# A hybrid attention layer on one core: TensorE's order pinned to the program through the attention stages

## The chip, the cores and the metric

The kernel runs on one core of a Trainium2 chip. The metric is the time of one execution on the device in microseconds (us), lower is better; the times shown are the median of several executions. Five engines work side by side, each in the order of its own queue: PE (TensorE: matmuls and transposes), DVE (VectorE), ACT (ScalarE), POOL (GpSimd) and SP (SyncE, which issues most DMAs). Where one needs another's result it waits on a semaphore.

## The reference

One decoder layer on x of 512 tokens by 2048, in float32. Each of the 8 FoX heads does softmax attention with a forgetting bias; the 8 NSA heads (two groups that share keys) mix three branches by sigmoid gates: attention over 31 compressed blocks, over selected blocks (all of them here, since 512 tokens have 8 blocks and 16 are taken) and over a window.

```python
def reference(x, ...):
    h = _rms_norm(x, attn_norm)
    x = x + _hybrid_mixer(h, ...)      # proj = h @ w_in, cut into qf, kf, vf, ff, qn, kc, vc, ks, vs, kw, vw, gt
    h = _rms_norm(x, ffn_norm)         # heads are RMS-normed, attended, concatenated, multiplied by w_out
    return x + (silu(h @ w_gate) * (h @ w_up)) @ w_down
```

## The kernel before, in words

Tokens lie along the free axis (512), features on the 128 partitions. Every float32 operand is split into a high and a low half, and every product is three matmuls: high by high, high by low and low by high (`mm3`, or the three calls in `unit`). ACT writes the high half (a copy that rounds), DVE the low one (`split`, `load_w`): so each weight part costs a load, an ACT pass and a DVE pass before PE can use all of it.

The work comes in four stages.

- *First projection* (5 to 50 us): x and the weights of kc and vc arrive in 16 steps `k`; each step makes `bigm` (x, split), `w0p` (the weight, split) and 12 matmuls of 512 columns into four banks `ps_first`. Squares of x are summed in `acc` for the norm; `ps_r` sums them over partitions, `rstd` is worked out by ACT and DVE, and `ps_rT` transposes it (`token_rstd`, called by `unload`).
- *Woven stage* (50 to 640 us): 20 units of the input projection (`ps_ks`, `ps_fg`, `ps_qn`, `ps_vs`, `ps_qf`, ...). `stream(units)` yields after every 6 matmuls of 256 columns, and `weave` steps side work in between at places that the list `plan` writes down: (first step, last step, how many, generator). Side work is the unloading of the first banks, the compressed keys and values (`z_kc`, `zkT`, `z_vc`), the gates with the cumulated forgetting (`ps_cum`), the normed and transposed heads (`nT_...`), and the attention branches: scores (`s_...`, `m_s`), transposed probabilities (`pT_...`, split into `pt_...`) and products with the values (`o_...`). Letters: f is FoX, s selected, w window; `s_f73` is head 7, query block 3.
- *Output projection* (640 to 664 us): `first_outs` fills `po0` and `po8`, with the last two heads woven in by a second `plan`.
- *The rest of the output projection, norm and feed-forward* (664 us to the end): here PE's order, ACT's and DVE's are already those of the program. The last pass ends in `finish(q, b)`, four times: DVE scales two banks by rstd (`t4_q`, `t62_q`; the profile drops the digits and calls them t) and adds them to the kept sums (`ca` is `y[1]`, `cb` is `y[0]`), whose halves are then stored.

A tile scheduler sets the order in each engine's queue. An instruction that went through `keep_in_program_order` (also as `pin`, while `pinned[0]` is set, and as `inorder` and `order0`) keeps its place among the other such instructions of its engine; one that did not is placed where the scheduler takes it to be ready. Before, PE's instructions of the first three stages are left to the scheduler, but for the warm-up and step k = 0; so are most of ACT's and DVE's, but for the weight halves and the first readers of projection banks. A psum bank of tag "g" or "t" has two buffers, so a matmul that starts a bank waits until the one two before has been read.

The code that the change touches:

## Time and profile before

| | |
|---|---|
| median of 3 runs | 2094.19 us (2093.47 to 2094.68) |
| profiled execution | 2093.31 us, of which the span of the trace is 2091.6 |
| PE busy | 99% of the span, 16935 matmuls and transposes |
| DVE busy | 79% |
| ACT busy | 46% |
| POOL busy | 9% |

Rows of the timeline read: start and duration in us, engine, line, operation, output<-input by the program's names without their numbers, shapes, xcount (several in one row), and in brackets the idle time ahead with the instruction that ended it. Rows of the list of waits read: engine, what waited, what it waited for, total us, times, longest. Matmuls overlap: their cost is the distance of their starts, not their duration.

### The profile page before, as it was taken

The page shows a single profiled execution, that of the slowest core. Times are in us where ns is not written, and L with a number is a line of the kernel's source. Part 1 is how long each engine was busy: PE and PEld are TensorE (multiplying, and loading weights), DVE is VectorE, ACT ScalarE, POOL GpSimd, SP SyncE. Part 2 cuts the span into 40 slices and gives each one's busy share as a digit, 9 for nine tenths or more (in the row PEclk, how much of TensorE's full clock was granted, in tenths as well). Part 3 has the DMA queues.
Part 4 walks back from the last instruction along what each step waited for, and adds up shares of the span by engine and source line. Part 5 has one row for each costly group of instructions (what it writes and reads, how often), then busy time and mean ns, then how long its engine had stood idle before and what let it go on. Part 6 is the DMA issues. An engine that isn't in the chain of part 4 may idle for free.

```text
span 2091.6 us, 40521 instructions
## 1 busy us (share of the span) xinstructions
PE 2079.4 (99%) x16935; PEld 2025.5 (97%) x16935; DVE 1648.8 (79%) x2437; ACT 966.6 (46%) x1226; POOL 181.8 (9%) x297
## 2 busy tenths in 40 slices
PE   9999999999999999999999999999999999999998
PEld 7999999999998888999999999999999999999998
DVE  6757667554456455999999999999999987889898
ACT  6445555444345334443344344433433455565553
POOL 1000000010010000111111111111111000000000
PEclk9999999999999999999999999999999999999999
DMA  5521211222223444667767767777777797579864
GB/s 202 172 87 51 71 52 61 81 95 81 94 82 106 151 143 141 174 198 193 198 190 187 194 189 196 197 180 204 189 185 200 243 337 248 153 240 331 290 179 139
DMA packets 113496, 350.58 MB, mean 168 GB/s; under 512 B 13592, under 2 KB 13848, under 8 KB 113312
## 3 DMA queue, kind: packets, MB, share of 16 engines
q1 hardware_dynamic: 85408, 270.98, 38.7%
q0 software_dynamic: 22144, 52.44, 14.2%
q10 hardware_dynamic: 5760, 24.57, 3.0%
q8 instruction: 132, 2.16, 0.4%
q14 instruction: 52, 0.43, 0.1%
HBM read 319.35 MB, written 74.73 MB: 188 GB/s over the span
## 4 chain that ended last, share of the span: by engine, by line
PE 93%; DVE 3%; ACT 2%; issue 1%; DMA 0%; SPq 0%; DVEq 0%; ACTq 0%
PE q L1182 39%; PE pd L1324 13%; PE pd L1329 6%; PE ps_qf L280 3%; PE ps_qf L283 3%; PE ps_qf L282 3%; PE po L166 3%; PE po L168 3%; PE po L167 3%; PE ps_vf L280 1%; PE ps_vf L283 1%; PE ps_vf L282 1%; PE ps_qn L280 1%; PE ps_qn L282 1%; PE ps_qn L283 1%
## 5 line engine op out<-in xcount | busy, mean ns | idle before, releaser
L83 ACT ACTIVATE bigm<-r 128x1792 fp32r<-128x1792 f32 x174 | 298.2, 1714 | 466.5 <-PE q L1182 296.9
L80 DVE TENSOR_TENSOR bigm<-r,bigm 128x1792 fp32r<-128x1792 f32 x174 | 351.4, 2020 | 11.6 <-ACT bigm L83 11.0
L80 DVE TENSOR_TENSOR r<-r 128x512 f32<-128x512 f32 x522 | 267.2, 512 | 29.2 <-DMA r<-wgu 16.8
L1182 PE MATMUL q<-bigm 128*128 128x256 f32 x1848 | 218.0, 277 | 0.1
L1182 PE MATMUL q<-forma,bigm 128*128 128x256 f32 x1848 | 216.9, 276 | 0.0
L1182 PE MATMUL q<-formy,bigm 128*128 128x256 f32 x1848 | 216.8, 276 | 0.0
L1182 PE MATMUL q<-formx,bigm 128*128 128x256 f32 x1848 | 216.8, 276 | 0.0
L1182 PEld LDWEIGHTS q<-bigm 128*128 128x128 f32 x1848 | 213.8, 188 | 0.3 <-DVE bigm L80 0.3
L1182 PEld LDWEIGHTS q<-forma,bigm 128*128 128x128 f32 x1848 | 213.1, 188 | 0.1
L1182 PEld LDWEIGHTS q<-formy,bigm 128*128 128x128 f32 x1848 | 212.9, 188 | 0.1
L1182 PEld LDWEIGHTS q<-formx,bigm 128*128 128x128 f32 x1848 | 212.9, 188 | 0.0
L125 POOL DMA_DIRECT2D wsum<-wdn x176 | 119.8, 687 | 863.9 <-ACT bigm L83 760.2
L280 PE MATMUL ps_qf<-wp_qf,bigm 128*128 128x256 f32 x512 | 145.1, 283 | 0.0
L283 PE MATMUL ps_qf<-wp_qf,bigm 128*128 128x256 f32 x512 | 142.3, 278 | 0.0
L282 PE MATMUL ps_qf<-wp_qf,bigm 128*128 128x256 f32 x512 | 142.3, 278 | 0.0
L1324 PE MATMUL pd<-bigm 128*128 128x256 f32 x1176 | 141.8, 276 | 0.0
L1324 PEld LDWEIGHTS pd<-bigm 128*128 128x128 f32 x1176 | 137.3, 188 | 0.0
L80 DVE TENSOR_TENSOR bigm<-wd,bigm 128x2048 fp32r<-128x2048 f32 (+1 forms) x64 | 110.2, 1723 | 12.2 <-ACT bigm L83 11.9
L83 ACT ACTIVATE bigm<-rawm 128x768 fp32r<-128x768 f32 (+2 forms) x72 | 65.9, 925 | 108.2 <-PE pd L1329 59.6
L166 PE MATMUL po<-bigm,wp_o 128*128 128x512 f32 x256 | 100.0, 390 | 0.0
L167 PE MATMUL po<-bigm,wp_o 128*128 128x512 f32 x256 | 99.8, 390 | 0.0
L168 PE MATMUL po<-bigm,wp_o 128*128 128x512 f32 x256 | 99.7, 390 | 0.0
(450 smaller groups left out, 4427.0 us busy)
## 6 DMA issues: line engine op xcount, KB each, us to landing
r<-wgu SPq DMA_DIRECT2D x174, 512.0 KB, 4.5
wsum<-wdn POOLq DMA_DIRECT2D x176, 256.0 KB, 4.9
rawm<-ad SPq DMA_DIRECT2D x44, 512.0 KB, 7.1
wd<-wdn SPq DMA_DIRECT2D x40, 512.0 KB, 6.0
wd<-wsum SPq DMA_DIRECT2D x40, 512.0 KB, 6.9
ad<-cb ACTq DMA_DIRECT2D x22, 896.0 KB, 5.7
rawm<-ad SPq DMA_DIRECT2D x44, 384.0 KB, 3.4
ws_qf<-win SPq DMA_DIRECT2D x32, 512.0 KB, 3.3
```

The costliest lines, as they stand in the source:

```text
L80: return pin(nc.vector.tensor_tensor(*args, op=op))
L83: return pin(nc.scalar.activation(*args, **kw))
L125: d = nc.gpsimd.dma_start(step[0], step[1], **step[2])
L166: nc.tensor.matmul(o, lh, rh, start=start, stop=False)
L167: nc.tensor.matmul(o, lh, rl, start=False, stop=False)
L168: nc.tensor.matmul(o, ll, rh, start=False, stop=stop)
L280: nc.tensor.matmul(o, xg[k][:, 0, c], wp[:, 0, w], start=(k == 0 and b == 0), stop=False, skip_group_check=True)
L282: nc.tensor.matmul(o, xg[k][:, 0, c], wp[:, 1, w], start=False, stop=False, skip_group_check=True)
L283: nc.tensor.matmul(o, xg[k][:, 1, c], wp[:, 0, w], start=False, stop=(k == NK - 1), skip_group_check=True)
L1182: nc.tensor.matmul(o, w[wp][:, fb, cs], a[:, xp, fa], start=(k == 0 and h == 0 and wp == 0 and xp == 0), stop=(g == NG - 1 and kk == 1 and ...
L1324: nc.tensor.matmul(b[q][k][:, h * 256:(h + 1) * 256], w[0][:, fb, q * P:(q + 1) * P], a[xp][:, fa], start=(j == 0 and h == 0 and xp == 0), ...
L1329: nc.tensor.matmul(b[q][k][:, h * 256:(h + 1) * 256], w[1][:, fb, q * P:(q + 1) * P], a[0][:, fa], start=False, stop=(j == NJ - 1), skip_g ...
```

## The change

It pins PE's order from the start of the woven stage to the end of the last attention branch: `mm3` and all matmuls and transposes of these stages now go through wrappers that keep the order of the program while `pe_pinned[0]` is set. Beside that ("all of the former"): x_0 and the first weights are loaded ahead of everything but the vector of gains; in steps k > 0 of the first projection, the split of x and w and the squares are pinned on ACT and DVE; `gneg` is worked out in step 1 instead of before the first step; the zeroing of a strip of `xb` is pinned; the first entry of `plan` starts one step later; and in `finish` the subtraction on `ca` goes to GpSimd for the first two passes, with the first addition on `cb` ahead of the store of `ca`.

```diff
+    pe_pinned = [False]
+
+    def pe_matmul(*args, **kw):
+        m = nc.tensor.matmul(*args, **kw)
+        return tc.keep_in_program_order(m) if pe_pinned[0] else m
+
+    def pe_transpose(*args, **kw):
+        m = nc.tensor.transpose(*args, **kw)
+        return tc.keep_in_program_order(m) if pe_pinned[0] else m
+
     def mm3(o, lh, ll, rh, rl, start, stop):
-        nc.tensor.matmul(o, lh, rh, start=start, stop=False)
+        pe_matmul(o, lh, rh, start=start, stop=False)
...
+    x0 = oxp.tile([P, T], F32, tag="ox", name="x_0", bufs=NOX)
     nc.scalar.dma_start(vt, vec)
+    nc.sync.dma_start(x0, xT[0])
+    early = oxp.tile([P, 5 * T], F32, tag="x5", name="early")
+    nc.sync.dma_start(early[:, :T], wfirst[0])
...
     gneg = ap_.tile([P, 2], F32, name="gneg")
-    nc.vector.tensor_scalar_mul(gneg[:, 0:1], v1(V_FQ), -SCALE)
-    nc.vector.tensor_scalar_mul(gneg[:, 1:2], v1(V_NQ), -SCALE)
...
-                nc.vector.tensor_scalar_mul(xb[:, 4 * T:4 * T + 16], ident[:, :16], 0.0)
+                inorder(nc.vector.tensor_scalar_mul(xb[:, 4 * T:4 * T + 16], ident[:, :16], 0.0))
...
-            nc.scalar.activation(sq, xs, AF.Square)
-            nc.vector.tensor_tensor(acc, acc, sq, op=OP.add)
+            pin(nc.scalar.activation(sq, xs, AF.Square))
+            pin(nc.vector.tensor_tensor(acc, acc, sq, op=OP.add))
...
-            split(t, xs, v1(V_AN + k))
+            pinned[0] = True
+            g = v1(V_AN + k)
+            pin(nc.scalar.activation(t[:, 0], xs, AF.Copy, scale=g))
+            pin(nc.vector.scalar_tensor_tensor(t[:, 1], xs, g, t[:, 0].bitcast(F32), op0=OP.mult, op1=OP.subtract))
             split(wp[:, :, :T], ws)
...
             square(k, xs)
+            if k == 1:
+                pin(nc.vector.tensor_scalar_mul(gneg[:, 0:1], v1(V_FQ), -SCALE))
+                pin(nc.vector.tensor_scalar_mul(gneg[:, 1:2], v1(V_NQ), -SCALE))
+            pinned[0] = False
...
-    plan = [(2, 30, 9, chain(unload(), windows("kc", V_PK))), (26, 42, 4, windows("vc", V_PV)),
+    plan = [(3, 30, 9, chain(unload(), windows("kc", V_PK))), (26, 42, 4, windows("vc", V_PV)),
...
+    pe_pinned[0] = True
     weave(stream(units), plan)
...
     weave(first_outs(), plan)
     run(rest)
+    pe_pinned[0] = False
...
-        tt(y[1], y[1], t4, op=OP.subtract)
-        fetch2(out[n + 1], y[1])
-        tt(y[0][:, :256], y[0][:, :256], t4[:, :256], op=OP.add)
+        pin((nc.gpsimd if q < 2 else nc.vector).tensor_tensor(y[1], y[1], t4, op=OP.subtract))
+        tt(y[0][:, :256], y[0][:, :256], t4[:, :256], op=OP.add)
+        fetch2(out[n + 1], y[1])
```

The number of instructions does not change on PE. Its order changes at some fifteen places; three of all the places, as the queues of the two kernels have them (line, operation, output<-input, shape, count):

PE, in the unit fg (the gate weights `wp_fg`, second part), before: seven matmuls of the compressed keys, then the first matmuls of four banks, which need the high half of the part alone, then the transposes of the normed ks0 and kw0, and only then a matmul with the low half (line 282).

```order
L528 MATMUL z_kc_860<-wp_kc0_863,xb_kc_701 128x256 x3
L528 MATMUL z_kc_860<-wp_kc1_905,xb_kc_701 128x256 x4
L280 MATMUL ps_fg0_827<-wp_fg_1_833,bigm_76 128x288
L280 MATMUL ps_fg1_828<-wp_fg_1_833,bigm_76 128x288
L280 MATMUL ps_fg2_829<-wp_fg_1_833,bigm_76 128x288
L280 MATMUL ps_fg3_830<-wp_fg_1_833,bigm_76 128x288
L340 MATMUL nT_ks0_986<-ident_124,t_ks0_533 128x128 x4
L340 MATMUL nT_kw0_1012<-ident_124,t_ks0_533 128x128 x4
L282 MATMUL ps_fg0_827<-wp_fg_1_833,bigm_76 128x288
```

The same place now; all wrapped matmuls have the line of the wrapper:

```order
L168 MATMUL ps_fg3_830<-wp_fg_0_742,bigm_76 128x288 x6
L168 MATMUL z_kc_860<-wp_kc0_863,xb_kc_701 128x256
L168 MATMUL ps_fg0_827<-wp_fg_1_833,bigm_76 128x288 x6
L168 MATMUL z_kc_860<-wp_kc0_863,xb_kc_701 128x256
L168 MATMUL ps_fg1_828<-wp_fg_1_833,bigm_76 128x288 x6
L168 MATMUL z_kc_860<-wp_kc0_863,xb_kc_701 128x256
L168 MATMUL ps_fg2_829<-wp_fg_1_833,bigm_76 128x288 x6
L168 MATMUL z_kc_860<-wp_kc1_905,xb_kc_701 128x256
```

One z_kc matmul stands ahead of the second part, and the second matmul of that part comes right behind its first; the other z_kc matmuls follow one by one, and nT_ks0 and nT_kw0 come two parts later.

PE, in the output projection, before: the transposes `nT_kf7` of the last key head, and the scores of its query block 3 (`s_f73`, three matmuls: high, and with the low halves), the two behind each other only in part.

```order
L340 MATMUL nT_kf7_7586<-ident_124,t_qf7_7248 128x128 x4
L166 MATMUL po8_7540<-bigm_76,wp_o8_0_7580 128x512
L465 MATMUL pT_f60_7607<-ident_124,p_f6_7127 128x128 x4
L167 MATMUL po8_7540<-bigm_76,wp_o8_0_7580 128x512
L166 MATMUL s_f73_7600<-qf7_7567 128x512
L168 MATMUL po8_7540<-bigm_76,wp_o8_0_7580 128x512
L166 MATMUL po8_7540<-bigm_76,wp_o8_0_7580 128x512
L167 MATMUL po8_7540<-bigm_76,wp_o8_0_7580 128x512
L168 MATMUL po8_7540<-bigm_76,wp_o8_0_7580 128x512
L166 MATMUL s_f72_7625<-qf7_7567 128x384
L166 MATMUL po8_7540<-bigm_76,wp_o8_0_7580 128x512
L167 MATMUL s_f73_7600<-qf7_7567 128x512
```

The same place now:

```order
L168 MATMUL po8_7540<-bigm_76,wp_o8_0_7580 128x512 x3
L172 MATMUL nT_kf7_7586<-ident_128,t_qf7_7248 128x128 x4
L168 MATMUL s_f73_7600<-qf7_7567 128x512 x3
L172 MATMUL pT_f60_7607<-ident_128,p_f6_7127 128x128 x4
L168 MATMUL po8_7540<-bigm_76,wp_o8_0_7580 128x512 x6
L168 MATMUL s_f72_7625<-qf7_7567 128x384 x3
L172 MATMUL pT_f61_7631<-ident_128,p_f6_7127 128x128 x4
```

The scores follow their transposes at once; pT_f60 and the matmuls of po8 stand behind them.

DVE, in the tail, before, in the first pass of `finish` and the start of the second:

```order
L80 TENSOR_TENSOR t4_0_22905<-pd30_1_21981,rstd_134 128x512
L80 TENSOR_TENSOR ca_8848<-ca_8848,t4_0_22905 128x512
L80 TENSOR_TENSOR cb_8846<-cb_8846,t4_0_22905 128x256
L80 TENSOR_TENSOR t62_0_22906<-pd30_0_21980,rstd_134 128x512
L80 TENSOR_TENSOR cb_8846<-cb_8846,t62_0_22906 128x512
L80 TENSOR_TENSOR t4_1_22941<-pd31_1_21983,rstd_134 128x512
```

And the end of POOL's queue now, behind the loads of x1:

```order
L1251 DMA ca_8848<-x1d13_7827 128x512
L1251 DMA cb_8846<-x1d14_7828 128x512
L1251 DMA ca_8848<-x1d15_7829 128x512
L1291 TENSOR_TENSOR ca_8848<-ca_8848,t4_0_22905 128x512
L1291 TENSOR_TENSOR ca_8848<-ca_8848,t4_1_22941 128x512
```

The subtractions on ca of the first two passes have left DVE's queue and are the last two instructions of POOL's.

## The prediction

> **What bounds the kernel now.** I read the head of the page first (span, busy time, granted clock, the chain that ended last), then the list of waits on PE, then a table of busy time by stretches, and last the timeline at every place where the change gives PE another order.

> ```profile
> span 2091.6 us, 40521 instructions
> PE 2079.4 (99%) x16935; PEld 2025.5 (97%) x16935; DVE 1648.8 (79%) x2437; ACT 966.6 (46%) x1226; POOL 181.8 (9%) x297
> PEclk9999999999999999999999999999999999999999
> PE 93%; DVE 3%; ACT 2%; issue 1%; DMA 0%; SPq 0%; DVEq 0%; ACTq 0%
> ...
> PE warm L753 <- DVE ones L210: 1.4, 1, 1.4
> PE ps_qn L282 <- DVE wp_qn L149: 1.0, 1, 1.0
> PE ps_first L168 <- DVE w0p L80: 0.7, 1, 0.7
> ...
> PE ps_rT L257 <- DVE rstd L218: 0.4, 1, 0.4
> PE pT_s L465 <- DVE pt_s L80: 0.3, 1, 0.3
> PE ps_qn L280 <- DVE vs L364: 0.2, 1, 0.2
> ...
> 50.00:120.00 70.00, 68.58 (x552) 66.50 (x551) 49.98 (x87) 34.22 (x61) 1.15 (x1) 1.00 0.50 163
> 664.00:2050.00 1386.00, 1385.88 (x11496) 1358.10 (x11496) 1208.41 (x1494) 626.76 (x537) 134.54 (x199) 1.00 0.70 204
> ```

> PE is busy 99% of the span at full granted clock and carries 93% of the chain. Its waits are few, and none before the tail is longer than 1.4 us. So the instruction count of PE (unchanged) sets the time, and all that the change can do up to the tail is to take away some of these few waits or to make new ones. In the table (length; busy time of PE, weight loads, DVE, ACT, POOL; clock; DMA) the feed-forward stretch from 664 to 2050 us has PE idle 0.1 us in 1386: it will only be shifted. DVE is busy 50.0 of 70 us in the stretch from 50 to 120: it is no bound, but its results often come just in time.

> **The change part by part.** The two orders of PE agree nearly everywhere. They differ at about fifteen places, and these have one form: before, PE had other ready work in front of an instruction whose input was late; in the order of the program that work stands behind it. What it costs is the moved work, as long as the late input comes at the same time as before. A projection matmul of 256 columns costs the distance of two starts, 0.113 us:

> ```profile
> 54.55 0.28 PE L280 MATMUL ps_ks<-wp_ks,bigm 128*128 128x256 f32 x1
> 54.66 0.28 PE L282 MATMUL ps_ks<-wp_ks,bigm 128*128 128x256 f32 x1
> 55.32 0.63 PE L257 MATMUL ps_rT<-ident,rstd 128*128 128x128 f32 x4 [0.38 <-DVE rstd L218]
> ...
> 54.48 0.69 DVE L218 TENSOR_TENSOR rstd<-rstd,tmp_r 128x512 f32<-128x512 f32 x1
> ```

> *rT.* The transposes of rstd come when DVE's row at 54.48 ends (55.17). Before, 32 matmuls lie between the sums of squares and them, now 18. The 14 that covered the wait are done afterwards: 14 x 0.113 = **+1.6**.

> *Gates and first compressed keys.* DVE makes the low half of the second part of the gate weights late, because a scaling of t_ks (1.22 us) stands ahead of it:

> ```profile
> 76.82 0.99 PE L528 MATMUL z_kc<-wp_kc,xb_kc 128*128 128x256 f32 x7
> 78.14 1.22 DVE L327 TENSOR_TENSOR t_ks<-t_ks,sn_ks 128x1024 f32<-128x1024 f32 x1
> 79.28 1.82 DVE L149 TENSOR_TENSOR wp_fg<-ws_fg,wp_fg 128x768 fp32r<-128x768 f32 x2
> 79.42 0.33 PE L340 MATMUL nT_ks<-ident,t_ks 128*128 128x128 f32 x1 [0.60 <-DVE t_ks L327]
> ```

> Until about 80.2 (79.28 and half of 1.82) PE had seven z_kc matmuls, four high-half gate matmuls and eight transposes to do. In the new order it can do one z_kc and one gate matmul. Six z_kc at 0.118 ((0.99 - 0.28)/6), three gate matmuls at 0.13 (0.113 x 288/256) and eight transposes at 0.10 (four took 0.63 in the rT row and one 0.33 here) move behind: 0.71 + 0.39 + 0.80 = **+1.9**. PE then stands still for some 3 us, in two pieces.

> *zkT, then the cumulated gates.* zkT waited 0.18 us for DVE; now 12 fewer matmuls lie ahead of it (1.36). ps_cum needs the triangle that DVE casts until 111.71; 5 of the 11 matmuls that covered this go (0.57). Together **+1.9**.

> ```profile
> 110.11 0.27 PE L544 MATMUL zkT<-ident,zks 64*128 64x64 f32 x1 [0.18 <-DVE zks L541]
> 111.28 0.43 DVE L620 CAST tri<-trif 128x512 fp32r<-128x512 f32 x1
> 154.47 1.26 DVE L452 TENSOR_SCALAR p_s<-p_s,st_s 128x512 f32<-128x512 f32 x4
> 209.17 0.30 PE L565 MATMUL m_s<-Kc,qn 128*128 128x64 f32 x1 [0.22 <-DVE st_s L442]
> 275.74 0.88 DVE L364 SCALAR_TENSOR_TENSOR vs<-ps_vs,rT,vs 128x256 fp32r<-128x256 f32 x2
> 276.28 0.39 PE L280 MATMUL ps_qn<-wp_qn,bigm 128*128 128x256 f32 x1 [0.25 <-DVE vs L364]
> ```

> *Third compressed score (row at 209.17).* It already waited; it now follows 12 instead of 24 matmuls: 12 x 0.113 = **+1.4**.

> *First part of qn6 (276.28).* Its bank is free when DVE has read vs. Before, three score matmuls of 512 columns, three of 384, three products of 256 and seven transposes ran ahead of it, now behind: 0.69 + 0.52 + 0.34 + 0.70 = 2.25, by the distances given here and below. In the new DVE order the reads of that bank stand together, without the masking of another score (some 0.7) between them: **+1.5**.

> *Small ones.* pT_s0 loses five covering matmuls (DVE's four scalings end at 155.73): 0.55. m_s1 loses three: 0.35. z_vc and m_s0: 0.3. **+1.2**.

> *Output projection with the last heads.*

> ```profile
> 644.17 1.22 DVE L327 TENSOR_TENSOR t_qf<-t_qf,sn_qf 128x1024 f32<-128x1024 f32 x1
> 648.96 0.74 DVE L138 SCALAR_TENSOR_TENSOR qf<-nT_kf,vt,qf 128x512 fp32r<-128x512 f32 x1
> 650.09 0.39 PE L167 MATMUL s_f<-qf 128*128 128x512 f32 x1
> 659.08 0.39 PE L167 MATMUL po<-bigm,wp_o 128*128 128x512 f32 x1
> 659.31 0.40 PE L168 MATMUL po<-bigm,wp_o 128*128 128x512 f32 x1
> 660.19 1.28 DVE L80 TENSOR_TENSOR pt_f<-pT_f,pt_f 128x512 fp32r<-128x512 f32 x2
> 660.93 0.44 PE L465 MATMUL pT_f<-ident,p_f 128*128 128x128 f32 x2
> ```

> Wide matmuls start 0.23 apart (659.08, 659.31). nT_qf stands two of them earlier: 0.45. s_f73 needs both halves of qf, the low one at 649.70 by DVE's row at 648.96; before, seven wide matmuls, a transpose group and single score matmuls ran there, now the three score matmuls come right behind nT_kf: I take 1.6, of 0.4 to 2.2. pT_f72 waits for a bank that DVE frees in the row at 660.19, behind three instead of nine wide matmuls: 6 x 0.23 = 1.4. Together **+3.45**.

> *First projection.* PE lost 0.7 us where DVE was late with w0p:

> ```profile
> 10.10 2.04 POOL L641 TENSOR_SCALAR nb<-nb 128x512 f32<-128x512 f32 x2
> 13.62 1.09 DVE L80 TENSOR_TENSOR w0p<-early,w0p 128x512 fp32r<-128x512 f32 x1
> 14.63 0.68 DVE L761 TENSOR_TENSOR acc<-acc,sq 128x512 f32<-128x512 f32 x1
> ```

> DVE's 128x512 takes 1.09 us while POOL works and 0.68 after it. The pinned order puts the weight split ahead of the sum of squares, and POOL's masks can start earlier, when DVE has little to do. I take **-0.9** (the wait and its restart); ends 0 and -1.1. The first loads go out in the same order as before; the squares that ACT now does in order have cover, since an x tile has 8 buffers.

> *Tail.* After the last matmul (about 2085.5) DVE works alone:

> ```profile
> 2077.16 0.69 DVE L80 TENSOR_TENSOR ca<-ca,t 128x512 f32<-128x512 f32 x1
> 2077.76 0.42 DVE L80 TENSOR_TENSOR cb<-cb,t 128x256 f32<-128x256 f32 x1
> 2085.30 0.28 PE L1347 MATMUL pd<-formx,bigm 128*128 128x256 f32 x1
> 2087.07 0.69 DVE L80 TENSOR_TENSOR t<-pd,rstd 128x512 f32<-128x512 f32 x1
> ```

> Two subtractions on ca go to POOL. DVE's rows follow each other without a gap there, so its chain gives up 2 x 0.60 (2077.16 to 2077.76) = 1.2; PE's end caps it at 2087.07 - 2085.58 = 1.5. POOL's price for this is not in the trace; its 128x512 tensor-scalar took 1.02 beside DVE (half of 2.04). While it works, DVE pays up to 0.41 an instruction (1.09 - 0.68), for three or four: the gain lies between 1.2 and -0.4. I take the middle, **-0.6**. DVE's t of the third pass also waits until POOL has read the first t; that is 4 us later. The store of ca now waits for POOL, long before the end. If DVE stood still through both POOL rows, 2 x 1.02 would be lost against 1.2, and the tail would be 0.8 longer. [...]

> *Sum.* 1.6 + 1.9 + 1.9 + 1.4 + 1.5 + 1.2 + 3.45 - 0.9 - 0.6 = +11.4. PE's later waits on DVE in the list (1.0, 0.3, 0.2 and a few like them, some 1.9 us) shrink if PE comes later and DVE doesn't; I take 1.9 off: **+9.5**. The profiled execution lasted 2093.31, 1.7 more than its span and 0.9 less than the median of the three runs, so 2094.2 + 9.5 = **2103.7**. Loads of weights are cast three buffers ahead and a later PE only gives them time.

> **The rivals.**
> *DVE runs ahead, and half of it vanishes.* While PE stands, ACT and DVE go on with weight splits that don't need PE. Each stall then makes the next input relatively early. The terms whose late input sits in DVE's queue behind such work (gates 1.9, third score 1.4, qn6 1.5, pT_f72 1.4, pT_s0 0.55) are 6.75; without them +2.75, or 2096.9, no change to be measured. For it: DVE has 20 us of slack in the 70 to 120. Against: in rT, zkT and s_f73 the late input is a chain from PE's own result, and it starts no earlier.
> *Faster.* If all inputs were there by the time the program calls for them, no new wait comes, and the old ones (0.7, 0.6, 0.4, 0.3, 0.2 and the 1.0) go, with 1.2 in the tail: -4.4, 2089.8. This decides only if DVE is earlier by 2 us at the gates and at 648.96, and nothing in the change takes work from its queue there.
> *The throttle.* The clock was granted in full in all 40 slices, with no wait above 1.4 us; the stands would now reach 3 us at the gates in two pieces, 1.5 to 2 at qn6 and s_f73. If the clock falls to half after such a stand, for as long again as PE stood there, these three lose half of 6.5 us more: 3.2, or 2106.9. Against it: behind each stand PE is at once busy again, and no row shows the clock react. [...]

> **How the numbers follow.** A measurement of this kernel can't tell less than 0.2%, 4.2 us: 2090.0 to 2098.4 is no change. The forecast (most of the sum stays, 2098.4 to 2106.5) 0.70; the sum in full or a little more, to 2108, 0.06; the throttle (some of it in the range) 0.04; half or less 0.14; faster 0.06. So slower 0.80, same 0.14, faster 0.06. The range 2096.5 to 2107.5 leaves out the faster case, the lower half of the "same" case and the throttle: some 0.17. Its lower end is the first rival; its upper end the sum without the 1.9 taken off, and with the tail and the first projection at nothing (2094.2 + 12.9 = 2107.1).

> **What would show it.** The list of waits on PE should now name rT with some 2 us (from 0.4), fg with 2 to 3 in two pieces, zkT, m_s and qn (on vs) with 1.3 to 2 each, s_f with 1.5 to 2, pT_f with 1.4, and ps_first should be gone from it. PE's busy time should stay at 2079, and the stretch from 664 to 2050 should keep its length. In the last stretch two POOL rows on ca should appear, with DVE rows near 1.1 beside them if they contend. I am wrong if DVE's rows at these places come earlier by as much as PE is, or if waits elsewhere shrink by more than 1.9.

## The result, and the profile after

The changed kernel takes 2109.22 us (median of 6 runs, 2108.55 to 2111.88) against 2094.19 before: ratio 1.0072, 95% interval 1.0062 to 1.0082. That is 15.0 us slower; 9.5 were forecast, and the range ended at 2107.5. The direction was right and the size was not. The profiled execution took 2109.01 with a span of 2107.3. In two of the experiments below, three executions (2140.45, 2126.98 and 2126.96 us) lay 1.7% above the fastest of their kernel at the same mean clock; the medians leave them out.

The head of the page of the changed kernel:

```profile
span 2107.3 us, 40543 instructions
PE 2082.9 (99%) x16935; PEld 2029.2 (96%) x16935; DVE 1649.4 (78%) x2435; ACT 968.0 (46%) x1226; POOL 182.9 (9%) x299
```

Its list of waits on PE (what waited, for what; total us, times, longest):

```profile
PE ps_qn L168 <- DVE vs L376: 2.6, 1, 2.6
PE ps_rT L269 <- DVE rstd L232: 2.0, 1, 2.0
PE ps_fg L168 <- DVE wp_fg L149: 1.9, 1, 1.9
PE m_s L168 <- DVE st_s L454: 1.9, 2, 1.6
PE zkT L172 <- DVE zks L553: 1.5, 1, 1.5
...
PE pT_f L172 <- DVE pt_f L80: 1.2, 1, 1.2
PE ps_qn L168 <- DVE wp_qn L149: 1.0, 1, 1.0
PE s_f L168 <- ACT qf L137: 0.8, 1, 0.8
PE s_f L168 <- DVE qf L138: 0.7, 1, 0.7
```

The new waits are those that were foretold, place by place, and ps_first is gone. But PE's busy time rose by 3.5 us with the same 16935 instructions, and the prediction had it staying at 2079. The table by stretches (length; busy time of PE, weight loads, DVE, ACT, POOL; granted clock; DMA) says where:

```profile
50.00:120.00 70.00, 63.15 (x493) 61.12 (x492) 47.99 (x86) 32.47 (x59) 1.15 (x1) 0.98 0.46 151
120.00:300.00 180.00, 173.56 (x1382) 168.43 (x1381) 115.05 (x299) 91.15 (x218) 8.96 (x15) 0.99 0.19 63
664.00:2050.00 1386.00, 1384.77 (x11437) 1354.99 (x11436) 1201.27 (x1498) 624.97 (x542) 134.25 (x201) 1.00 0.69 203
```

The clock fell to 0.98 and 0.99 on the mean. The forty slices of the page hid it: a slice is 53 us. The same table, cut where the clock rows of the trace change, in pairs (a stretch of 3.41 us, the first one cut short by 0.05, and the next one), and two more stretches of that grid:

```profile
78.00:81.36 3.36, 0.97 (x5) 0.55 (x5) 3.26 (x8) 1.58 (x3) 0.00 (x0) 1.00 0.22 78
81.36:84.77 3.41, 3.41 (x16) 3.41 (x16) 0.70 (x1) 0.27 (x1) 0.00 (x0) 0.50 0.71 216
282.75:286.16 3.41, 0.97 (x8) 0.97 (x9) 1.45 (x4) 2.28 (x6) 0.00 (x0) 1.00 0.00 0
286.16:289.57 3.41, 3.41 (x19) 3.41 (x18) 1.62 (x2) 1.31 (x2) 0.00 (x0) 0.50 0.13 19
112.08:115.49 3.41, 1.87 (x15) 1.58 (x13) 3.35 (x14) 1.43 (x8) 1.00 (x1) 1.00 0.43 153
214.48:217.89 3.41, 1.83 (x16) 1.63 (x15) 2.85 (x13) 1.19 (x5) 0.00 (x0) 1.00 0.36 125
```

Behind the stands at the gates (81 us) and at the first part of qn6 (286 us) the clock was halved for 3.41 us each. By the granted 0.50, as an estimate, PE did in them what takes 1.7 us: twice 1.7 us lost. (From 286.52 us one projection matmul took 0.42 us and four 1.06, so they start 0.213 apart, against 0.113 at full clock; by these it is 1.6.) Behind the stands at zkT (112) and the third compressed score (214), where PE was busy 1.83 us or more of the 3.41, it was not.

For the terms I took the distance in time between the same projection matmul in both traces, at points where PE has done the same work in both. The loss grows by: first projection -0.53; rT +1.42; gates +3.5 (of which 1.7 clock); zkT and ps_cum +1.9; z_vc, m_s0, pT_s0, m_s1 together +1.2; third compressed score +1.4; qn6 +4.1 (1.7 clock); from there to the output projection -0.4; output projection +3.45; feed-forward and tail -0.4. These give the 15.7 us between the two spans, within 0.1.

### The profile page after: what moved, and what is told of

It reads as the page before. It is cut to its first block, busy times and chain, and to the rows that moved or that the text cites. A ratio compares the mean times of both kernels' runs of the same rounds, so it can differ in the third digit from the quotient of the medians.

```text
span 2107.3 us, 40543 instructions
## 1 busy us (share of the span) xinstructions
PE 2082.9 (99%) x16935; PEld 2029.2 (96%) x16935; DVE 1649.4 (78%) x2435; ACT 968.0 (46%) x1226; POOL 182.9 (9%) x299
## 4 chain that ended last, share of the span: by engine, by line
PE 94%; DVE 3%; ACT 2%; issue 1%; DVEq 0%; ACTq 0%
PE q L1205 40%; PE pd L1347 13%; PE ps_qf L168 8%; PE po L168 8%; PE pd L1352 6%; PE ps_vf L168 4%; PE ps_qn L168 3%; PE ps_first L168 2%; PE ps_ks L168 2%; PE o_s L168 1%; PE ps_fg L168 1%; PE o_f L168 1%; PE s_f L168 1%; PE s_s L168 0%; PE s_w L168 0%
## 5 line engine op out<-in xcount | busy, mean ns | idle before, releaser
L80 DVE TENSOR_TENSOR bigm<-r,bigm 128x1792 fp32r<-128x1792 f32 x174 | 351.4, 2019 | 8.5 <-ACT bigm L83 8.3
L80 DVE TENSOR_TENSOR r<-r 128x512 f32<-128x512 f32 x522 | 267.2, 512 | 32.8 <-DMA r<-wgu 20.7
L168 PE MATMUL ps_qf<-wp_qf,bigm 128*128 128x256 f32 x1536 | 187.3, 280 | 0.0
L168 PEld LDWEIGHTS ps_qf<-wp_qf,bigm 128*128 128x128 f32 x1536 | 180.1, 188 | 0.0
L168 PE MATMUL po<-bigm,wp_o 128*128 128x512 f32 x768 | 176.6, 390 | 0.0
L168 PEld LDWEIGHTS po<-bigm,wp_o 128*128 128x128 f32 x768 | 143.5, 188 | 29.1
L1347 PE MATMUL pd<-bigm 128*128 128x256 f32 x1176 | 141.8, 276 | 0.0
L1347 PEld LDWEIGHTS pd<-bigm 128*128 128x128 f32 x1176 | 137.2, 188 | 0.0
L80 DVE TENSOR_TENSOR bigm<-wd,bigm 128x2048 fp32r<-128x2048 f32 (+1 forms) x64 | 110.3, 1723 | 12.2 <-ACT bigm L83 11.8
L168 PE MATMUL ps_qn<-wp_qn,bigm 128*128 128x256 f32 x768 | 103.2, 285 | 3.6 <-DVE vs L376 2.6
L168 PEld LDWEIGHTS ps_qn<-wp_qn,bigm 128*128 128x128 f32 x768 | 95.5, 191 | 4.2 <-DVE vs L376 2.8
```

What stands on the lines that cost most here:

```text
L80: return pin(nc.vector.tensor_tensor(*args, op=op))
L168: m = nc.tensor.matmul(*args, **kw)
L1347: nc.tensor.matmul(b[q][k][:, h * 256:(h + 1) * 256], w[0][:, fb, q * P:(q + 1) * P], a[xp][:, fa], start=(j == 0 and h == 0 and xp == 0), ...
```

## The experiments

**The change without the pinning.** PE then stands in the order of the kernel before, instruction by instruction; the loads, the order on ACT and DVE, and the tail stay changed.

```diff
-    pe_pinned[0] = True
+    pe_pinned[0] = False
     weave(stream(units), plan)
```

> The changed kernel without the pinning of PE; all the rest of the change stays. PE then has the very order of the kernel before. If the pinning alone costs the time (theory: cover moved behind late inputs, 11.5 to 12.5 us, and two stretches of 3.4 us at half clock, 3.4 us), this kernel is as fast as before or 0.5 us faster (the first projection gained 1.0 and lost 0.5 at its start): 2093 to 2094.5, and no stretch at half clock before the end. Rival: the other edits carry part of the loss; then it lies above 2097.

Measured: 2092.54 us (median of 11, 2091.83 to 2093.56), before in the same session 2093.97; ratio 0.9990, interval 0.9981 to 0.9999. The waits on PE are those of the kernel before but for the first projection's:

```profile
PE warm L168 <- DVE ones L224: 1.4, 1, 1.4
PE ps_qn L168 <- DVE wp_qn L149: 1.0, 1, 1.0
...
PE ps_rT L269 <- DVE rstd L232: 0.4, 1, 0.4
```

The clock is not halved before the last matmul (the mean of the whole span is 0.999, in the changed kernel 0.998). So the order of PE alone makes the loss, some 16.7 us (2109.22 - 2092.54), and the rest of the change is worth 1.4 us to the good (by the interval, 0.2 to 4.0), a little more than expected. This version is the fastest here, ahead of both kernels; the last experiment, a variant of it, is level with it.

**The pinning alone**, on the kernel before, with the plan's first entry left at step 2.

```diff
+    pe_pinned[0] = True          # with the wrappers, on the kernel before
     weave(stream(units), plan)
...
     run(rest)
+    pe_pinned[0] = False
```

> The kernel before with PE pinned through the same stages and nothing else of the change; the plan's first entry stays at step 2, so rT stands six matmuls (0.7 us) earlier than in the changed kernel. Theory: 15.5 + 0.7 over before, 2109 to 2111.5. Rival, that pinning hurts only together with the other edits: under 2104.

Measured: 2111.95 us (2109.66 to 2115.16), ratio 1.0084 (1.0072 to 1.0096): +18.0, a little over the expected range. rT waits longer, as it should with six matmuls fewer ahead of it:

```profile
PE ps_rT L172 <- DVE rstd L228: 2.6, 1, 2.6
```

Its profiled execution (2115.16, the slowest of the five) has four halved stretches instead of two: half clock followed rT and zkT as well (PE was busy 1.23 and 1.30 us of the 3.41 ahead). At 1.7 each that is 6.8 us of its 21. The five executions line up by the mean clock of each: 2109.66 us at 0.999, 2111.62 and 2111.95 at 0.998, 2113.22 at 0.997, 2115.16 at 0.996.

**Idle matmuls in the two stands behind which the clock fell.**

```diff
+    def fill(n, tag):
+        f = ps.tile([P, NB, P], F32, tag=tag, name="fill")
+        for _ in range(n):
+            pe_matmul(f, ones, ones[:, None, :].to_broadcast([P, NB, P]), start=True, stop=True)
...
+                        if (name, k, g, b) == ("qn6", 0, 0, 0):
+                            fill(10, "m")
...
+                        if (j, kk, g, b) == (1, 0, 0, 0) and groups == 4:
+                            fill(8, "o")
```

> The changed kernel with idle matmuls of 128x512 on ones, 8 of them behind the first matmul of the second gate part and 10 ahead of the first matmul of qn6, in spare psum banks: they fill 1.8 of the 2.1 and 2.3 of the 2.6 us in which PE stood there, and change nothing else. Theory (these two stands trip the throttle, and each costs 1.7 us): no half-clock stretch at 81 and 286 us, 3.4 us less than the changed kernel, 2105.8. Rival (the clock rows cost nothing, PE waits for DVE anyway): the time stays at 2109.2.

Measured: 2109.66 us (2106.14 to 2110.24), no gain: by its total, the rival. Its trace (of an execution of 2108.79) says otherwise. At the gates it gains some 1.6 us on the changed kernel and at qn6 as much, and the clock holds there. But it loses nearly the same in two other places:

```profile
111.42:114.83 3.41, 1.56 (x9) 1.11 (x10) 2.82 (x10) 1.23 (x5) 1.15 (x1) 1.00 0.46 154
114.83:118.24 3.41, 3.41 (x16) 2.76 (x15) 0.68 (x1) 0.00 (x0) 0.00 (x0) 0.50 0.03 5
213.82:217.23 3.41, 1.83 (x16) 1.63 (x15) 2.85 (x11) 1.19 (x5) 0.00 (x0) 1.00 0.18 61
217.23:220.64 3.41, 3.41 (x19) 3.41 (x18) 2.31 (x11) 0.90 (x3) 0.00 (x0) 0.50 0.25 97
```

The stands at zkT and at the third score are as long as in the changed kernel (1.7 us each). At zkT the stretch of 3.41 us lies 1.1 us later against them than there, and so takes in the stand at ps_cum too: PE is busy 1.56 us of it instead of 1.87. At the third score the stretch holds the whole stand in both, with 1.83 us of busy time in both, and the clock fell here and not there. So a stand alone did not decide, and neither did 1.83 us of busy time. One of the five executions had a mean clock of 1.000, so no halved stretch before the tail (one takes 0.0008 off the mean of the span): it took 2106.14 us, where the theory said 2105.8; the four others, at 0.998 and 0.999, took 2108.79 to 2110.24.

**The same for all the larger stands of the pinned stages.**

```diff
+        fill(8, "o")
         o = ps.tile([P, T], F32, tag="m", name="ps_rT")
...
+            fill(6, "o")
             zkT = ps.tile([P, 64], F32, tag="t", name="zkT", bufs=2)
...
+        if h == 2:
+            fill(6, "t")
         s = live["m"][:, 3 * P:3 * P + 64]
```

> As e3_fill, with idle matmuls also ahead of rT (8), zkT (6) and the third compressed score (6): no stand of PE in the pinned stages is left longer than some 1.0 us. In e3_fill the two half-clock stretches at 81 and 286 us went, and two others came, at 115 and 217 us, in an execution whose 3.41 us windows lay otherwise. Theory (a window of 3.41 us of which PE stands some 2.0 or more halves the clock for the next): no half-clock stretch at all before the end, 3.4 us under the changed kernel, 2105.5, and a narrower spread of the runs. Rival (the time is lost otherwise): 2109.

Measured: 2106.12 us (2105.54 to 2109.26; four of the five within 0.6), 3.1 less than the changed kernel; ratio to before 1.0060 (1.0047 to 1.0074). The mean clock of its span is 1.000, and there is no halved stretch up to the last matmul:

```profile
50.00:120.00 70.00, 68.20 (x528) 64.83 (x527) 49.11 (x87) 32.69 (x60) 1.15 (x1) 1.00 0.49 153
120.00:300.00 180.00, 177.19 (x1408) 170.99 (x1407) 115.30 (x301) 91.02 (x217) 8.97 (x15) 1.00 0.20 63
```

The idle matmuls compute nothing that is used, and the kernel is faster with them. The one run at 2109.26 had a mean clock of 1.000 too, so its 3 us are not the clock's; what they are is open, and the narrower spread that was expected did not come. What remains over the kernel before, about 12 us, is the moved cover, by the terms listed with the result.

**Stands of chosen length**, where the changed kernel otherwise hardly waits: PE is busy 339.71 of the 340 us from 300 to 640.

```diff
+    GAPS = {"qf2": 2, "vf2": 3, "qf3": 4, "qf4": 5, "vf4": 6, "qf5": 8, "qf6": 3, "vf6": 4}
+
+    def gap(n, name):
+        f = ps.tile([P, T], F32, tag="m", name=f"gap_{name}")
+        t = ap_.tile([P, T], FR, tag="fr", name=f"gt_{name}")
+        pe_matmul(f, ones, ones[:, None, :].to_broadcast([P, NB, P]), start=True, stop=True)
+        for _ in range(n):
+            inorder(nc.scalar.activation(t, f, AF.Copy))
+        f2 = ps.tile([P, T], F32, tag="m", name=f"gap2_{name}")
+        pe_matmul(f2, ones, t, start=True, stop=True)
```

> The changed kernel with eight stands of PE put in between 400 and 640 us, where it otherwise never waits: in each, PE waits for 2, 3, 4, 5, 6, 8, 3 and 4 copies of 128x512 on ACT (0.6 us each), so for some 1.5 to 5 us. Theory: the clock is halved for 3.41 us after each window of 3.41 us in which PE stood for 2.0 us or more, so after the stands of 3.0 us and more always, after those of 2.1 us sometimes, after 1.5 never, and it stays halved for as many windows as stay idle. Rival, a stand must last 3.41 us by itself: half clock only after the ones of 4, 5 us. Rival, any stand over 1.5 us does it: after all eight.

Measured in one execution: 2159.99 us. The stands lasted 2.2, 2.8, 3.5, 4.1, 4.7, 6.0, 3.2 and 3.5 us, 0.7 longer than expected of the shortest. The clock fell behind all eight: for one stretch of 3.41 us behind those of 2.2, 2.8, 3.5 (the first) and 3.2, and for two behind the four others (4.1, 4.7, 6.0 and the second 3.5). The shortest, and the one of 4.1:

```profile
433.00:436.42 3.42, 1.35 (x10) 0.98 (x9) 1.23 (x1) 2.14 (x3) 0.00 (x0) 1.00 0.00 0
436.42:439.83 3.41, 3.41 (x19) 3.41 (x18) 0.00 (x0) 0.00 (x0) 0.00 (x0) 0.50 0.47 154
...
525.16:528.58 3.42, 1.14 (x9) 0.82 (x8) 1.42 (x2) 2.54 (x6) 0.19 (x1) 1.00 0.00 0
528.58:531.99 3.41, 1.73 (x7) 1.64 (x8) 0.00 (x0) 1.56 (x3) 0.00 (x0) 0.50 0.45 154
531.99:535.40 3.41, 3.41 (x18) 3.41 (x18) 0.00 (x0) 0.00 (x0) 0.00 (x0) 0.50 0.00 0
```

That a stand must last 3.41 us by itself is refuted: 2.2 was enough here. Since none came out at 1.5, this run does not tell apart the theory from the rival "any stand over 1.5 us"; the stands of 1.7 at zkT in the changed kernel and of 2.1 at rT, behind which the clock held, do: not every stand over 1.5 us was followed by half clock. The first put-in stand cost 4.4 us on the whole: 0.45 for its two matmuls, 2.25 of standing, and 1.7 (half of 3.41, an estimate) at half clock.

**The changed kernel, twice more.**

> The changed kernel once more, unchanged, for another execution with its clock rows. Theory: the windows of 3.41 us run on their own, so they lie otherwise against the program; the stands of PE are the same to 0.05 us, but which of them meet a window with 2.0 us or more of standing differs. Time = 2105.6 + 1.7 for each halved window before the end (2109.0 with two). Rival, the throttle answers to the stand and not to its place in a window: again just after the gates and qn6, 2109.0.

> The changed kernel a third time, with the same expectation as e9_again: 2105.6 + 1.7 for each halved window, and the halved windows right behind those windows in which PE stood 2.0 us or more.

Measured: 2108.89 and 2108.69 us, both with two halved stretches. In the second these lie behind the gates and qn6, as in the first profile. In the other one they lie behind the gates and the third compressed score; qn6 escaped, because its stand fell across two stretches, so that PE was busy 2.00 us of the one:

```profile
213.60:217.01 3.41, 1.82 (x16) 1.62 (x15) 2.85 (x10) 1.20 (x6) 0.00 (x0) 1.00 0.19 52
217.01:220.42 3.41, 3.41 (x18) 3.41 (x18) 2.23 (x11) 0.72 (x2) 0.00 (x0) 0.50 0.26 102
281.86:285.27 3.41, 2.00 (x14) 1.72 (x12) 2.06 (x9) 1.58 (x5) 0.00 (x0) 1.00 0.00 0
```

The same kernel, the same stands, other victims: which stand half clock followed differed with its place in the grid, and the grid lay otherwise in each of the three executions (the first halved stretch began at 81.36, 80.48 and 80.68 us). That refutes the rival, that the stand alone decides.

**Pinned in the woven stage only.**

```diff
     weave(stream(units), plan)
+    pe_pinned[0] = False
```

> The changed kernel with the pinning ended before the output projection: nT_qf, s_f and pT_f of the last heads stand as before. Theory, stalls add up place by place: 3.45 us less than the changed kernel, 2105.8. Rival, that the output projection has slack behind it that swallows the stalls: 2108 or more.

Measured: median 2108.03 us of five runs, scattered from 2105.22 to 2111.38; ratio 1.0064 (1.0051 to 1.0077). The median lies at the edge of the rival's range; with that scatter it can't decide. The profiled execution (2105.55, two halved stretches at the places of the changed kernel) is 3.49 us shorter in its span, and but for 0.2 all of it is gained between 640 and 690 us, where PE no longer waits:

```profile
640.00:664.00 24.00, 24.00 (x165) 21.73 (x164) 16.05 (x24) 12.71 (x21) 0.00 (x0) 1.00 0.32 108
```

Like against like, in executions with the same two halved stretches, the output projection's part is the 3.45 expected, and nothing behind it swallows it. The clock explains the scatter in part: the runs of 2108.03 and 2111.38 had a mean clock of 0.996, which in the pinning alone went with four halved stretches, and the profiled one 0.998. But the run of 2110.37 had 0.998 as well, so the rest is open.

**Cover put back at two places, PE still pinned.**

```diff
-    plan = [(3, 30, 9, chain(unload(), windows("kc", V_PK))), (26, 42, 4, windows("vc", V_PV)),
-            (34, 62, 32, keys_), (66, 105, 55, chain(keys_, gates(), compress("vc")))]
+    plan = [(6, 30, 9, chain(unload(), windows("kc", V_PK))), (26, 42, 4, windows("vc", V_PV)),
+            (34, 62, 32, keys_), (70, 105, 55, chain(keys_, gates(), compress("vc")))]
```

> The changed kernel with two numbers of the plan changed: the unloading (with rT) starts at step 6 instead of 3, and the side work that begins with zkT at step 70 instead of 66. PE stays pinned, but 18 more projection matmuls (2.0 us) come ahead of rT and 30 (3.4 us) ahead of zkT. Theory (the loss is the cover that was taken away): PE's stands at rT (2.1) and zkT with ps_cum (1.7 + 0.7) go, 4.3 us less than the changed kernel, 2105; the stands at the gates and qn6 and their half clock stay. Rival (a later rT and zkT only move the wait to what hangs on them): 2108 or more.

Measured: 2106.88 us (2104.06 to 2108.51), ratio 1.0060 (1.0047 to 1.0072): 2.3 less than the changed kernel, half of what was expected. In its trace rT, zkT and ps_cum wait no more. By the same projection matmul it leads the changed kernel by 2.0 us at 57 us of that kernel's time. The gates take back 1.2 (the waits of fg on ACT 1.1 and 1.0 us, from 0.5 and 0.4), so that 0.8 are left at 86 us. zkT and ps_cum then bring 2.3, and wp_qn takes 0.5; at 147 us the lead is 2.6. (At 118 us it is 4.7, but there this run still has side work ahead of it that the changed kernel has done: its ps_cum comes only 0.4 earlier.)

```profile
PE ps_qn L168 <- DVE wp_qn L149: 1.5, 1, 1.5
...
PE ps_fg L168 <- ACT wp_fg L148: 1.1, 1, 1.1
PE ps_fg L168 <- ACT sq_ks L327: 1.0, 1, 1.0
```

So the cover is the cause at rT and zkT, and the rival has its part: of the 4.3 us that the two places gave, 1.7 went at places behind them. That the later unloading makes these inputs late is likely, but no run isolates it. (The profiled execution lost 2.1 us more at 1690 to 1730 us, in the feed-forward stage; its total is not used.)

**The tail.**

```diff
-        pin((nc.gpsimd if q < 2 else nc.vector).tensor_tensor(y[1], y[1], t4, op=OP.subtract))
+        pin(nc.vector.tensor_tensor(y[1], y[1], t4, op=OP.subtract))
```

> e1_former_alone (PE not pinned) with the two subtractions on ca left on DVE. If POOL's part is worth the 0.25 us that the trace of e1_former_alone shows between PE's last matmuls and the end, this lies at 2092.8; if it is worth the 0.6 of the prediction, at 2093.1; if it costs (DVE slowed beside POOL), at 2092.2 or less.

Measured: 2092.64 us (median of nine, 2091.74 to 2094.62), ratio to before 0.9994 (0.9984 to 1.0003), against 2092.54 and 0.9990 with POOL: not to be told apart. POOL's part in the tail is worth less than these runs can show.

## Why the prediction was wrong

*What bounds, and the places: right.* PE's waits appeared where they were foretold, and the feed-forward stretch was only shifted (with the tail, 0.4 us were won back).

*The sizes of the moved cover: right, but for qn6.* Foretold and found: rT 1.6 and 1.4; gates 1.9 and 1.8 (without the clock); zkT and ps_cum 1.9 and 1.9; third score 1.4 and 1.4; small ones 1.2 and 1.2; output projection 3.45 and 3.45. This counting, matmuls moved times the distance of their starts, held to 0.2 us at six places of seven. (The 1.6 of s_f73 within the last was a choice from 0.4 to 2.2, and that it came out is in part luck.) For qn6, 1.5 was foretold and 2.4 found without the clock. The step that failed there is "the reads of that bank stand together, so it comes free earlier". They do stand together in DVE's queue, but each waits for ACT's high half, and ACT waits for DVE's read before it. The first row is of the kernel before, the others of the changed one:

```profile
274.71 0.48 DVE L364 SCALAR_TENSOR_TENSOR vs<-ps_vs,rT,vs 128x256 fp32r<-128x256 f32 x1 [0.95 <-ACT vs L363]
...
283.63 0.48 DVE L376 SCALAR_TENSOR_TENSOR vs<-ps_vs,rT,vs 128x256 fp32r<-128x256 f32 x1 [0.95 <-ACT vs L375]
284.14 0.84 ACT L375 ACTIVATE vs<-ps_vs,rT 128x256 fp32r<-128x256 f32 x2 [0.55 <-DVE vs L376]
284.65 0.88 DVE L376 SCALAR_TENSOR_TENSOR vs<-ps_vs,rT,vs 128x256 fp32r<-128x256 f32 x2 [0.54 <-ACT vs L375]
285.19 0.98 PE L168 MATMUL ps_qn<-wp_qn,bigm 128*128 128x256 f32 x6 [2.58 <-DVE vs L376]
```

From the first of these reads to the second it is 1.03 us before (274.71 to the row at 275.74 in the prediction) and 1.02 now. The masking that stood between them had filled a wait; taking it out freed nothing.

*The step that took 1.9 off the sum failed.* The later waits on DVE were to shrink as PE came later. They did not: the wait on wp_qn is 1.0 in both lists. Its chain starts at PE itself: from ACT's first read of PE's bank to DVE's late weight half it is 4.96 us before and after. The timeline before:

```profile
134.39 0.60 ACT L313 ACTIVATE t_qn<-ps_qn 128x512 f32<-128x512 f32 x1
139.35 2.51 DVE L149 TENSOR_TENSOR wp_qn<-ws_qn,wp_qn 128x1024 fp32r<-128x1024 f32 x2
```

And after:

```profile
140.92 0.60 ACT L325 ACTIVATE t_qn<-ps_qn 128x512 f32<-128x512 f32 x1
145.88 2.50 DVE L149 TENSOR_TENSOR wp_qn<-ws_qn,wp_qn 128x1024 fp32r<-128x1024 f32 x2
```

Here a later PE only shifted that loop. Of the others, pT_s keeps its 0.3 and nT_qn its 0.2. What came back between qn6 and the output projection was 0.4 us. The first rival, that DVE runs ahead and half of the loss vanishes, failed too: the gates and the third score came in nearly in full, and qn6 with more.

*The throttle was given 0.04, and it is 3.4 of the 5.5 us that were missing.* The step that failed is that the sum has no term for the clock and the range leaves it out. The rival's price came near (3.2), but by luck: it took half of three stands, that at s_f73 among them, and what came was 3.41 us at half clock (1.7 us lost) behind each of two, and none at s_f73. It was held unlikely because PE is busy again behind each stand and no row read of the kernel before showed the clock react. The rows of the changed kernel show it: the halved stretches last 3.41 us, and those of one execution begin a whole number of 3.413 us apart (60.0 from 81.36 to 286.16). Ahead of both, PE was still busy some 1.0 us of the 3.41. Of the full-clock windows of that grid read in these profiles between the start of the woven stage and the tail, half clock followed each in which PE was busy 1.56 us or less by the profile (0.83 the least), and none with 1.87 or more. Near 1.83 (the third score's stand, whole in its window) it followed in two executions of the eight that had it so. One window in the tail of the run with all the larger stands filled does not fit; the next one, without any matmul, was still at full clock (the mean of that span is 1.000, and a halved stretch takes 0.0008 off):

```profile
2096.95:2100.36 3.41, 1.49 (x14) 1.29 (x12) 3.34 (x6) 0.00 (x0) 0.00 (x0) 1.00 0.44 166
```

So the line between 1.56 and 1.87 is no exact one.

*First projection and tail.* -0.9 foretold, -0.5 found: the w0p wait went, but POOL's masks now run when DVE splits the first weights (POOL's last one from 4.74 to 5.41 us), which took 0.97 us for 0.69 (at 5.01 before; the prediction had them run where DVE has little to do). The tail's POOL instruction took 1.53 us, where 1.02 was the nearest row, and beside it one DVE instruction took 1.07 us, for 0.69 before (at 2081.81), and the one ahead of it 0.68:

```profile
4.98 0.97 DVE L791 TENSOR_TENSOR w0p<-early,w0p 128x512 fp32r<-128x512 f32 x1
...
2096.12 1.53 POOL L1291 TENSOR_TENSOR ca<-ca,t 128x512 f32<-128x512 f32 x1 [1.26 <-DVE t L80]
2097.13 1.07 DVE L80 TENSOR_TENSOR cb<-cb,t 128x512 f32<-128x512 f32 x1
```

In sum: +9.5 forecast, 1.9 that was not absorbed, 0.9 at qn6, 0.4 in the first projection and 3.4 of half clock make 16.1. The drift of -0.4 brings them to the 15.7 between the two profiled spans; between the medians it is 15.0.

## What to carry to other kernels

Pinning an engine to the order of the program gives up whatever work stood in front of its late inputs: count that work at each place where the two orders differ. Here it was the loss to 0.2 us at six places of seven. Take nothing off for later waits before the trace shows that their chain starts at another engine than the one that is late. And a sum with stands of PE of some 2 us needs a term for the clock: here half clock for 3.41 us, some 1.7 us lost, followed stands of 1.9 and 2.6 us (by the list of waits) that left PE busy some 1.0 us of a stretch of 3.41. Where the cover can't be put back, a few idle matmuls kept the clock here at 1.000 on the mean, 3.1 us under the changed kernel.
